# Weaving the second block's attention into its dense products by another measure, and turning stick-breaking weights from fp32r copies

## The chip, the cores and the metric

The kernel runs on one core of one Trainium2 chip. Its time is the device time of one launch in microseconds (us): median 1038.97 us over three runs (1035.66 to 1039.84). Each profile is one execution on the chip, taken by the hardware profiler. Five engines work side by side: TensorE (PE in the rows, PEld for its weight loads), VectorE (DVE), ScalarE (ACT), GpSimd (POOL) and SyncE (SP), which here only issues transfers. Each works through its own instructions in order.

## The reference

Two transformer-like blocks on a sequence of 512 tokens, width 1024, all in float32. The change touches the attention of the second block alone:

```python
h = rmsnorm_2(x, g_norm1) * (1.0 + sc1) + sh1
q_sb, k_sb, v_sb, q_ca, k_ca, v_ca = split(h @ w_in)
# 8 heads of stick-breaking attention, in blocks of 128 queries
z = einsum('bqhd,bkhd->bhqk', qb, kb) * d ** -0.5
log_1m_beta = where(strict, log_sigmoid(-z), 0.0)
suffix = cumsum(log_1m_beta, reverse=True) - log_1m_beta
w = where(strict, exp(log_sigmoid(z) + suffix), 0.0);  o_sb = w @ v
# 8 heads of banded softmax attention with a relative bias
q_ca, k_ca = rmsnorm_2(q_ca), rmsnorm_2(k_ca)
o_ca = softmax(q_ca @ k_ca * d ** -0.5 + bias) @ v
x = x + gt1 * (concat(o_sb, o_ca) @ w_o)
```

The factors sh1, sc1, gt1 and their later twins are slices of `silu(c) @ w_ada + b_ada`, a product of one row with a 1024 x 6144 matrix: the modulation. Everything in the block reads x, which the first block makes.

## The kernel before

A float32 weight is split into two fp32r halves, `wh` and `wl` (a cast on ScalarE, line 133, and a subtraction on GpSimd or VectorE, line 130), and each dense product is three matrix products (lines 152 to 154). The dense work of the second block is a generator, `dense2`: the q and k columns of one pair of heads after the other (`qk2_sb`, `qk2_ca`), two chunks of v (`v2_chunk`), and at last the products with w_o (`wo_first`), in the order of the table `DENSE`. The attention is a second generator, `attn2`. It goes through the 8 pairs of heads in the order 0, 1, 4, 2, 5, 3, 6, 7; pairs 0 to 3 are stick-breaking, 4 to 7 softmax. Each pair is 8 units: two heads, each with four query blocks i = 0 to 3, whose rows hold 128, 256, 384 and 512 keys.

A stick-breaking unit (`stick`) takes its scores z on TensorE (lines 452, 453, and a mask product, 960), goes through three ScalarE passes (lines 961 to 963), three VectorE passes (964, a reversed running sum in 966, 967) and an exponential on ScalarE (968). A softmax unit (`soft`) takes a VectorE pass (975), an exponential (977) and a scaling (978, 979). The `turn` of a unit, three units later (`LAG`), transposes its blocks on TensorE (line 987, in float32), and ScalarE or VectorE copies the result (990, 992). After a pair's last turn `pv2` multiplies by v (923).

TensorE's order is fixed by hand, by the planner `weave`: it keeps a clock, lets each stream go on only when what it asked for is ripe (`LAT_...`), and among the ready streams picks the one with the least `spent / share`. Both streams charge the TensorE time of what they issue; the share of attention is `SHARE2 = 0.55`. A gate keeps dense work at most two pairs ahead of attention. The order on the other engines is set by a scheduler from the dependencies.

The modulation comes in eighths: `ada` loads two row blocks of 512 KB and adds them up on VectorE (lines 219 and 221, 16 operations for the slice gt1, v = 2), called by `ada_step` after every attention unit until the list is done; `ada_end` closes a half on TensorE (238).

Of the kernel before, what the change touches and what calls it, by code (L numbers as in the profile page):

```python
# [9 lines left out]
F32R = mybir.dt.float32r  # L10
# [16 lines left out]


SHARE1 = 0.35
SHARE2 = 0.55  # L30
TURN2 = 4
TURN1 = 4
WOUT_DVE = (1, 2, 4, 6)
ORDER = (0, 1, 4, 2, 5, 3, 6, 7)
LAST_SB = 3
DENSE = (1, "v2", 4, 2, 5, 3, "v3", 6, 7)
LAT_CA = 6000.0
LAT_SM = 3200.0
LAT_SB = (4000.0, 5500.0, 6500.0, 7500.0)
LAT_CM = (3200.0, 3800.0, 4400.0, 5000.0)  # L40
LAT_QK = 2600.0
LAT_SQ = 5000.0
LAT_ADA = 6500.0
# [5 lines left out]
def f(ap):  # L49
    return ap.bitcast(F32)  # L50
# [3 lines left out]
def hybrid_then_adaln_block(ctx, tc, a, out, tap=None):  # L54
    nc = tc.nc
    pe, act, dve, pool, sp = nc.tensor, nc.scalar, nc.vector, nc.gpsimd, nc.sync

    consts = ctx.enter_context(tc.tile_pool(name="consts", bufs=1))
# [6 lines left out]
    def bank():  # L65
        return pbank.tile([128, 512], F32, name="ps", tag="ps", bufs=8)
# [4 lines left out]
    clk = [0.0]  # L71

    def mark(name, late=LAT_QK):
        done[name] = clk[0] + late
# [4 lines left out]
    def ripe_at(need):  # L79
        if need is None:  # L80
            return 0.0
        return need[1] if need[0] == "@" else done.get(need, float("inf"))

    def weave(*streams):


        share, streams = [x[0] for x in streams], [x[1] for x in streams]
        n = len(streams)
        spent, need, live = [0.0] * n, [None] * n, [True] * n
        while any(live):  # L90
            up = [q for q in range(n) if live[q]]
            ready = [q for q in up if ripe_at(need[q]) <= clk[0]]
            if not ready:
                clk[0] = min(ripe_at(need[q]) for q in up)
                assert clk[0] < float("inf"), need
                continue
            q = min(ready, key=lambda q: spent[q] / share[q])
            need[q] = None
            try:
                got = next(streams[q])  # L100
            except StopIteration:
                live[q] = False
                continue
            if isinstance(got, tuple):
                need[q] = got
            else:
                spent[q] += got
                clk[0] += got
# [4 lines left out]
    def sm(shape, name, bufs=4):  # L113
        return small.tile(shape, F32, name=name, tag=name, bufs=bufs)
# [53 lines left out]
    pool.memset(eps_c, EPS)  # L168
    ident = consts.tile([128, 128], F32, name="ident")
    make_identity(nc, ident)  # L170
    ones_f = consts.tile([128, 128], F32, name="ones_f")
    pool.memset(ones_f, 1.0)
    sel = consts.tile([128, 8], F32R, name="sel")
# [87 lines left out]
    def ada_step(n=1, wait=True):  # L261
        for _ in range(n):
            if ada_due and (clk[0] >= ada_due[0][2] or not wait):
                ada_end()
            if todo and not (ada_due and todo[0][1] % 4 == 0):
                ada(*todo.pop(0))
# [11 lines left out]
    def wt(shape, tag, dt=F32):  # L278
        return work.tile(shape, dt, name=tag, tag=tag, bufs=BUFS[tag])
# [199 lines left out]
    def attn1():  # L479
# [60 lines left out]
        for n in range(len(units) + LAG + 1):  # L540
            if n < len(units):
# [3 lines left out]
                yield scores(p, i, e)  # L545
                ripe[n] = clk[0] + LAT_SM
            if 0 <= n - LAG < len(units):
# [207 lines left out]
    for t in range(4):  # L755
        x = resid.tile([128, D], F32, name="xr", tag="xr", bufs=4)
# [160 lines left out]
    def pv2(p, W):  # L917
        po = bank()
        for j in range(4):
            n = 512 - 128 * j  # L920
            for e in range(2):
                hc = slice(128 * p + 64 * e, 128 * p + 64 * e + 64)
                pe.matmul(po[64 * e:64 * e + 64, 128 * j:], V2[j][:, hc], W[e][:, j, 128 * j:], start=j == 0, stop=j == 3)  # L923
            yield 0.89 * n
        if MX.get(p // 4) is not None:
            act.copy(MX[p // 4][:, p % 4, :], po)
        else:
            x = wt([128, 512], "T")
            act.copy(x, po)
            sp.dma_start(mx_d[p % 4], x)  # L930
            away.append(p % 4)
        mark(("mx", p), 1500.0)

    away = []
    st, P = {}, {}
# [10 lines left out]
    def att2_steps():  # L946
        def products(p, i, e, stop):
            if i == 0:
                st[p, e] = wt([128, 4, 512], "PT"), wt([128, 4, 512], "Y") if p < 4 else None
            L = 128 * (i + 1)  # L950
            N = max(L, 256)
            ps = bank()
            mm_packed(ps[:, :N], QK2[p], e, slice(128 * i, 128 * i + 128), slice(0, N), stop)
            x = P[p, i, e] = st[p, e][1][:, i, :] if p < 4 else wt([128, 512], "T")
            return ps[:, :L], x[:, :L], 2 * N / 2.4

        def stick(p, i, e):

            z, x, t = products(p, i, e, False)
            pe.matmul(z[:, 128 * i:], identb, mkb, start=False, stop=True)  # L960
            act.activation(x, z, AF.Abs)
            act.activation(x, x, AF.Exp, scale=-1.0)
            act.activation(x, x, AF.Ln, bias=1.0)
            dve.scalar_tensor_tensor(x, z, 0.0, x, op0=OP.max, op1=OP.add)
            back = x[:, ::-1]
            dve.tensor_tensor_scan(back, ones_f[:, :1].to_broadcast([128, z.shape[1]]), back, 0.0, op0=OP.mult, op1=OP.add)  # L966
            dve.tensor_tensor(x, z, x, op=OP.subtract)
            act.activation(x, x, AF.Exp)
            return t + 56

        def soft(p, i, e):
            s, x, t = products(p, i, e, True)
            nmx, sums = sm([128, 1], "nmx"), sm([128, 1], "sums")
            bs = strips[2 * (p - 4) + e]
            dve.tensor_tensor_reduce(x, s, bs[:, 384 - 128 * i:512], scale=-1.0, scalar=3.0e38,
                                     op0=OP.add, op1=OP.min, accum_out=nmx)
            act.activation(x, x, AF.Exp, scale=-1.0, bias=nmx, accum_out=sums)
            dve.reciprocal(sums, sums)
            dve.tensor_scalar(x, x, sums, None, op0=OP.mult)
            return t  # L980

        def turn(p, i, e):
            x = P.pop((p, i, e))
            PT = st[p, e][0]
            pt = bank().rearrange("p (j n) -> p j n", j=4)
            for j in range(i + 1):
                pe.transpose(pt[:, j, :], x[:, 128 * j:128 * j + 128], ident)  # L987
            o = PT[:, :i + 1, 128 * i:128 * i + 128]
            if i % 2:
                act.copy(o, pt[:, :i + 1, :])  # L990
            else:
                dve.tensor_copy(o, pt[:, :i + 1, :])
            return 110 * (i + 1)

        return stick, soft, turn

    def attn2():
        MX[0] = wt([128, 4, 512], "V")
        stick, soft, turn = att2_steps()
        units = [(p, i, e) for p in ORDER for e in range(2) for i in range(4)]  # L1000
        LAG = 3
        ripe = {}
        for n in range(len(units) + LAG + 1):
            if n < len(units):
                p = units[n][0]
                if n % 8 == 0:
                    yield ("qk2", p)
                yield (stick if p < 4 else soft)(*units[n])
                ada_step()
                ripe[n] = clk[0] + (LAT_SB if p < 4 else LAT_CM)[units[n][1]]  # L1010
                if n % 8 == 7:
                    mark(("att", p), 800.0)
            if 0 <= n - LAG < len(units):
                yield at(ripe[n - LAG])
                yield turn(*units[n - LAG])
            m = n - LAG - 1
            if m >= 0 and m % 8 == 7:
                p = units[m][0]
                yield at(clk[0] + LAT_PV2)
                yield from pv2(p, [st[p, e][0] for e in range(2)])  # L1020
                if p == LAST_SB:
                    MX[1] = wt([128, 4, 512], "Y")
                    for q in away:
                        sp.dma_start(MX[1][:, q, :], mx_d[q])

    def dense2():
        load_strips(0, f(h2l[1][:, 3, 384:385]))
        jobs = {"v2": lambda: v2_chunk(2), "v3": lambda: v2_chunk(3)}
        for x in DENSE:
            yield from with_norms(jobs[x]() if x in jobs else qk2_sb(x) if x < 4 else qk2_ca(x - 4))  # L1030
# [34 lines left out]
    for c in range(2):  # L1065
        for t in range(2, 4):
            run(v2_tile(c, t, vw[c]))
    weave((SHARE2, attn2()), (1.0, dense2()))
    if tap: tap("sb1", MX[0][:, 1, :]); tap("ca1", MX[1][:, 1, :])
# [23 lines left out]
    for t in range(4):  # L1093
        x = resid.tile([128, D], F32, name="xr", tag="xr", bufs=4)
# [37 lines left out]
    got = {}  # L1132
# [63 lines left out]
    for tag, n in [("PT", 1), ("Y", 1), ("V", 1), ("Y", 3), ("h", 2)]:  # L1196
        for _ in range(n):
            t = wt([128, 4, 512], tag) if tag != "h" else hpool.tile([128, 4, 512], F32, name="hid", tag="h", bufs=4)
# [202 lines left out]
```

## Time and profile before

| | |
|---|---|
| median of three runs | 1038.97 us |
| the profiled execution | 1035.2 us |
| its span, first to last instruction | 1033.5 us |
| TensorE, VectorE, ScalarE busy | 999.8, 654.9, 567.1 us |
| mean granted TensorE clock | 0.992 of full speed |

The profiled execution is 3.8 us below the median of the runs; 1.7 us of it lie outside the span. The page gives, for each engine, the share of the span in which it was busy. Since it is a mean over stages, the stage that the change touches (443 to 656 us, from the first stick-breaking scores to the last pair's product with v) is read by itself below.

### The profile page before, as it was taken

The numbers are of one execution on the slowest core, as the hardware profiler recorded it, in microseconds if no ns is written. First come the engines' busy times: TensorE is split into PE (matmuls) and PEld (weight loads), VectorE is DVE, ScalarE is ACT, GpSimd is POOL, SyncE is SP. The second block draws the span as 40 slices with busy tenths as digits, with TensorE's granted clock in tenths as the row PEclk, the third lists the DMA queues.
The fourth block names the chain that finished last, engine by engine and source line by source line (L and its number), as shares of the span: only waits on it lengthen the run. The fifth ranks groups of instructions, "written<-read, shape, count | busy, mean of one in ns | idle before, by whom it ended". The sixth has DMA issues, their size and how long they took to land.

```text
span 1033.5 us, 15410 instructions
## 1 busy us (share of the span) xinstructions
PE 999.8 (97%) x5870; PEld 850.0 (82%) x5870; DVE 654.9 (63%) x1204; ACT 567.1 (55%) x1098; POOL 294.5 (28%) x136
## 2 busy tenths in 40 slices
PE   8999999999999999997999989999999999999997
PEld 7987877868888888976777867799999998888886
DVE  5465867964636669678678778669578746611114
ACT  5456654445455455566689888347567773322330
POOL 4222214313333066003212134122122232333320
PEclk9999999999999999998999999999999999999999
DMA  8442534435455675335222244432244335732302
GB/s 232 121 143 62 139 97 123 122 113 153 112 153 163 218 230 166 99 102 164 67 68 81 72 129 128 147 104 81 55 111 123 85 128 175 194 112 84 101 20 82
DMA packets 136060, 125.55 MB, mean 121 GB/s; under 512 B 8141, under 2 KB 112417, under 8 KB 135986
## 3 DMA queue, kind: packets, MB, share of 16 engines
q1 hardware_dynamic: 135986, 124.56, 41.2%
q8 instruction: 46, 0.75, 0.3%
q14 instruction: 28, 0.23, 0.1%
HBM read 119.82 MB, written 4.73 MB: 121 GB/s over the span
## 4 chain that ended last, share of the span: by engine, by line
PE 83%; DVE 7%; ACT 5%; issue 3%; POOL 1%; DMA 1%; DVEq 0%; POOLq 0%; ACTq 0%
PE ps L152 21%; PE ps L153 20%; PE ps L154 20%; PE ps L1184 4%; PE ps L1186 4%; PE ps L1185 4%; PE ps L987 2%; PE ps L923 1%; PE ps L452 1%; PE ps L453 1%; DVE ada L221 1%; PE ps L533 1%; PE ps L515 1%; PE ps L238 1%; DVE Y L966 1%
## 5 line engine op out<-in xcount | busy, mean ns | idle before, releaser
L130 POOL TENSOR_TENSOR wl<-wr,wh 128x1024 fp32r<-128x1024 f32 x99 | 247.4, 2502 | 616.9 <-ACT wh L133 611.7
L133 ACT CAST wh<-wr 128x1024 fp32r<-128x1024 f32 x130 | 135.8, 1047 | 103.4 <-PE ps L153 40.5
L152 PE MATMUL ps<-hh,wh 128*128 128x512 f32 (+1 forms) x352 | 129.8, 369 | 0.0
L153 PE MATMUL ps<-hl,wh 128*128 128x512 f32 (+1 forms) x352 | 125.0, 355 | 0.0
L154 PE MATMUL ps<-hh,wl 128*128 128x512 f32 (+1 forms) x352 | 124.8, 355 | 0.0
L152 PE MATMUL ps<-wh,T 128*128 128x512 f32 x256 | 100.4, 392 | 0.0
L153 PE MATMUL ps<-wl,T 128*128 128x512 f32 x256 | 100.3, 392 | 0.0
L154 PE MATMUL ps<-wh,T 128*128 128x512 f32 x256 | 99.9, 390 | 0.0
L221 DVE SCALAR_TENSOR_TENSOR ada<-wr,vc,ada 128x512 f32<-128x512 f32 x84 | 83.0, 988 | 6.4 <-DMA wr<-in_w_ada_dram 5.1
L152 PEld LDWEIGHTS ps<-hh,wh 128*128 128x128 f32 x352 | 66.3, 188 | 19.7 <-issue 10.8
L154 PEld LDWEIGHTS ps<-hh,wl 128*128 128x128 f32 x352 | 66.4, 189 | 9.7
L153 PEld LDWEIGHTS ps<-hl,wh 128*128 128x128 f32 x352 | 66.4, 189 | 7.7
L154 PEld LDWEIGHTS ps<-wh,T 128*128 128x128 f32 x256 | 48.1, 188 | 10.8
L152 PEld LDWEIGHTS ps<-wh,T 128*128 128x128 f32 x256 | 48.1, 188 | 10.6
L153 PEld LDWEIGHTS ps<-wl,T 128*128 128x128 f32 x256 | 48.1, 188 | 10.2
L130 DVE TENSOR_TENSOR wl<-wr,wh 128x1024 fp32r<-128x1024 f32 x31 | 40.9, 1319 | 24.1 <-ACT wh L133 24.0
L152 PE MATMUL ps<-h2h,wh 128*128 128x512 f32 (+1 forms) x144 | 54.3, 377 | 0.0
L1186 PE MATMUL ps<-QK,wl 128*128 128x256 f32 x192 | 53.6, 279 | 0.0
L1184 PE MATMUL ps<-QK,wh 128*128 128x256 f32 x192 | 53.5, 279 | 0.0
L1185 PE MATMUL ps<-PT,wh 128*128 128x256 f32 x192 | 53.3, 278 | 0.0
L154 PE MATMUL ps<-h2h,wl 128*128 128x512 f32 (+1 forms) x144 | 52.9, 367 | 0.0
L153 PE MATMUL ps<-h2l,wh 128*128 128x512 f32 (+1 forms) x144 | 52.7, 366 | 0.0
(412 smaller groups left out, 2687.1 us busy)
## 6 DMA issues: line engine op xcount, KB each, us to landing
wr<-in_w_in_dram SPq DMA_DIRECT2D x64, 512.0 KB, 4.7
wr<-in_w_dram SPq DMA_DIRECT2D x64, 512.0 KB, 4.1
wr<-in_w_ada_dram SPq DMA_DIRECT2D x48, 512.0 KB, 4.4
wr<-in_w_out_dram SPq DMA_DIRECT2D x12, 512.0 KB, 4.3
wr<-in_w_o_dram SPq DMA_DIRECT2D x12, 512.0 KB
xr<-in_x_dram SPq DMA_DIRECT2D x8, 512.0 KB
wr<-in_w_up_pool_dram SPq DMA_DIRECT2D x8, 256.0 KB
wr<-in_w_up_attn_dram SPq DMA_DIRECT2D x8, 256.0 KB, 4.2
```

Of the source, the lines that this page charges most:

```text
L130: (eng or pool).tensor_tensor(dst, raw, f(hi), op=OP.subtract)
L133: act.copy(dst_hi, raw)
L152: pe.matmul(ps, lh, rh, start=start, stop=False, **go)
L153: pe.matmul(ps, lh, rl, start=False, stop=False, **go)
L154: pe.matmul(ps, ll, rh, start=False, stop=stop, **go)
L221: dve.scalar_tensor_tensor(acc, raw[:, q, :], cs, acc, op0=OP.mult, op1=OP.add)
L238: pe.matmul(ps[:, j:j + 1], acc[:, 128 * j:128 * j + 128], ones_f[:, :1], start=True, stop=True)
L452: pe.matmul(ps, A[e][:, sa], B[e][:, sb], start=True, stop=False)
L987: pe.transpose(pt[:, j, :], x[:, 128 * j:128 * j + 128], ident)
L1184: pe.matmul(ps, wh, bh, start=first and k == 0, stop=False, **go)
L1185: pe.matmul(ps, wh, bl, start=False, stop=False, **go)
L1186: pe.matmul(ps, wl, bh, start=False, stop=k == 3, **go)
```

## The change

Five things are edited. The shares and delays of the planner change. A unit of attention now advances the clock by its TensorE time as before, but charges its stream a pace by block (`PACE_SB` 1100 to 2900 ns, `PACE_CM` 750 to 1600 ns), the turns charge nothing, and the share is 0.8. The second v chunk moves behind pair 6 in `DENSE`. The modulation waits until the seventeenth unit and takes a step at every third unit. And the weights of a stick-breaking unit are copied after their exponential, by a transfer from one SBUF tile to another of type fp32r (a third tile per head of the tag `Y`, whose four buffers stay); the turn reads the copy with an fp32r identity.

```diff
-SHARE2 = 0.55
+SHARE2 = 0.8
+PACE_SB = (1100.0, 1700.0, 2300.0, 2900.0)
+PACE_CM = (750.0, 1000.0, 1300.0, 1600.0)
...
-DENSE = (1, "v2", 4, 2, 5, 3, "v3", 6, 7)
+DENSE = (1, "v2", 4, 2, 5, 3, 6, "v3", 7)
...
-LAT_SB = (4000.0, 5500.0, 6500.0, 7500.0)
-LAT_CM = (3200.0, 3800.0, 4400.0, 5000.0)
+LAT_SB = (6500.0, 8000.0, 9000.0, 10000.0)
+LAT_CM = (4500.0, 5000.0, 5500.0, 6500.0)
...
-            if isinstance(got, tuple):
+            if isinstance(got, tuple) and got[0] == "$":
+                clk[0] += got[1]
+                spent[q] += got[2]
+            elif isinstance(got, tuple):
                 need[q] = got
...
+    identr = consts.tile([128, 128], F32R, name="identr")
+    dve.tensor_copy(identr, ident)
...
-            yield 0.89 * n
+            yield "$", 0.89 * n, 100.0
...
-                st[p, e] = wt([128, 4, 512], "PT"), wt([128, 4, 512], "Y") if p < 4 else None
+                st[p, e] = [wt([128, 4, 512], "PT")] + ([wt([128, 4, 512], "Y"), wt([128, 4, 512], "Y", F32R)] if p < 4 else [])
...
             act.activation(x, x, AF.Exp)
+            sp.dma_start(f(st[p, e][2][:, i, :z.shape[1]]), x)
...
-                pe.transpose(pt[:, j, :], x[:, 128 * j:128 * j + 128], ident)
+                c = slice(128 * j, 128 * j + 128)
+                if p < 4:
+                    pe.transpose(pt[:, j, :].bitcast(F32R), st[p, e][2][:, i, c], identr)
+                else:
+                    pe.transpose(pt[:, j, :], x[:, c], ident)
...
-                yield (stick if p < 4 else soft)(*units[n])
-                ada_step()
+                t = (stick if p < 4 else soft)(*units[n])
+                yield "$", t, (PACE_SB if p < 4 else PACE_CM)[units[n][1]]
+                if n >= 16 and n % 3 == 0:
+                    ada_step()
...
-                yield turn(*units[n - LAG])
+                yield "$", turn(*units[n - LAG]), 0.0
```

What moves is shown at three places. The first is VectorE at the very start of the stage, the first head of pair 0; `Y` are a unit's values, `ada` the running sum of the modulation. Before:

```order
L964 SCALAR_TENSOR_TENSOR Y_4324<-ps_4325,Y_4324 128x128
L246 SCALAR_TENSOR_TENSOR scl_91<-mod_90,vc_89 128x4
L219 TENSOR_SCALAR ada_4366<-wr_4364,vc_89 128x512
L966 SCALAR_TENSOR_TENSOR Y_4324<-ones_f_83,Y_4324 128x128
L221 SCALAR_TENSOR_TENSOR ada_4366<-wr_4364,vc_89,ada_4366 128x512
L967 TENSOR_TENSOR Y_4324<-ps_4325,Y_4324 128x128
L964 SCALAR_TENSOR_TENSOR Y_4324<-ps_4369,Y_4324 128x256
L221 SCALAR_TENSOR_TENSOR ada_4366<-wr_4383,vc_89,ada_4366 128x512
L966 SCALAR_TENSOR_TENSOR Y_4324<-ones_f_83,Y_4324 128x256
L221 SCALAR_TENSOR_TENSOR ada_4366<-wr_4383,vc_89,ada_4366 128x512
L967 TENSOR_TENSOR Y_4324<-ps_4369,Y_4324 128x256
L964 SCALAR_TENSOR_TENSOR Y_4324<-ps_4387,Y_4324 128x384
```

The same place in the changed kernel, whose lines 964, 966 and 967 are 972, 974 and 975:

```order
L972 SCALAR_TENSOR_TENSOR Y_4326<-ps_4328,Y_4326 128x128
L974 SCALAR_TENSOR_TENSOR Y_4326<-ones_f_85,Y_4326 128x128
L975 TENSOR_TENSOR Y_4326<-ps_4328,Y_4326 128x128
L972 SCALAR_TENSOR_TENSOR Y_4326<-ps_4367,Y_4326 128x256
L974 SCALAR_TENSOR_TENSOR Y_4326<-ones_f_85,Y_4326 128x256
L975 TENSOR_TENSOR Y_4326<-ps_4367,Y_4326 128x256
L972 SCALAR_TENSOR_TENSOR Y_4326<-ps_4388,Y_4326 128x384
L449 SCALAR_TENSOR_TENSOR QK_4350<-ps_4357,QK_4350 64x512
```

No operation of the modulation stands among the first units any more; the packing of the next pair's q (line 449) comes between them.

The second place is VectorE inside pair 4, at the change from its first head to its second; `T` are a softmax unit's values and `Z` the bias strips. Before (line 975 is the first pass of a softmax unit, 978 and 979 its scaling, 992 a copy after a turn):

```order
L975 ISA T_5062,nmx_5063<-ps_5059,Z_4336 128x512
L975 ISA nmx_5063 128x1
L978 RECIPROCAL sums_5048<-sums_5048 128x1
L992 COPY PT_5013<-ps_5075 128x128
L979 TENSOR_SCALAR T_5046<-T_5046,sums_5048 128x384
L942 MEMSET Z_5314 64x64
L978 RECIPROCAL sums_5064<-sums_5064 128x1
L979 TENSOR_SCALAR T_5062<-T_5062,sums_5064 128x512
L975 ISA T_5092,nmx_5093<-ps_5089,Z_4341 128x128
```

The changed kernel there, with lines 984, 987, 988, 1005 and 229 for 975, 978, 979, 992 and 221:

```order
L984 ISA T_5044,nmx_5045<-ps_5041,Z_4340 128x512
L984 ISA nmx_5045 128x1
L1005 COPY PT_4951<-ps_5051 128x128
L229 SCALAR_TENSOR_TENSOR ada_5032<-wr_5089,vc_91,ada_5032 128x512
L987 RECIPROCAL sums_5046<-sums_5046 128x1
L984 ISA T_5068,nmx_5069<-ps_5065,Z_4345 128x128
L984 ISA nmx_5069 128x1
L988 TENSOR_SCALAR T_5044<-T_5044,sums_5046 128x512
L984 ISA T_5082,nmx_5083<-ps_5079,Z_4345 128x256
L984 ISA nmx_5083 128x1
L229 SCALAR_TENSOR_TENSOR ada_5032<-wr_5089,vc_91,ada_5032 128x512
```

All 16 operations of the modulation now stand between the units of pairs 4, 2 and the first of pair 5.

The third place is SyncE's queue of transfers around pair 2; `wr` are weights, `Z` bias strips. Before:

```order
L139 DMA wr_5644<-in_w_in_2_dram 128x4x256
L139 DMA wr_5810<-in_w_in_2_dram 128x8x128
L139 DMA wr_5867<-in_w_in_2_dram 128x8x128
L139 DMA wr_5925<-in_w_in_2_dram 128x8x128
L944 DMA Z_5314<-in_band_dram 64x64
```

The changed kernel, where line 977 is the new copy of a unit's weights:

```order
L977 DMA Y_5129<-Y_5128 128x128
L217 DMA wr_5609<-in_w_ada_2_dram 128x2x512
L145 DMA wr_5631<-in_w_in_2_dram 128x8x128
L145 DMA wr_5690<-in_w_in_2_dram 128x4x256
L951 DMA Z_5205<-in_band_dram 128x448
L951 DMA Z_5210<-in_band_dram 128x448
L952 DMA Z_5210<-in_band_dram 64x64
L977 DMA Y_5129<-Y_5128 128x256
```

The 32 copies share the queue with the loads; the second copy of pair 2 stands behind six of them.

## Rows read from the trace of the kernel before

**Rows 1.** The page: span, and busy time of each engine.

```profile
span 1033.5 us, 15410 instructions
PE 999.8 (97%) x5870; PEld 850.0 (82%) x5870; DVE 654.9 (63%) x1204; ACT 567.1 (55%) x1098; POOL 294.5 (28%) x136
```

**Rows 2.** Windows: length, each engine's busy time (instructions), clock, DMA share, GB/s.

```profile
443.00:520.50 77.50, 67.72 (x386) 56.38 (x385) 58.16 (x95) 54.01 (x112) 20.91 (x8) 0.96 0.41 116
520.50:568.30 47.80, 47.39 (x280) 36.79 (x278) 39.71 (x106) 42.81 (x98) 8.96 (x4) 1.00 0.23 72
568.30:650.70 82.40, 75.40 (x416) 59.45 (x414) 64.99 (x151) 65.56 (x140) 25.23 (x10) 0.98 0.37 113
```

**Rows 3.** TensorE's waits, 443 to 656 us: total, times, longest.

```profile
PE ps L453 <- DVE lz L448: 4.4, 1, 4.4
PE ps L238 <- DVE Y L967: 2.5, 1, 2.5
...
PE ps L987 <- DVE T L979: 1.7, 1, 1.7
```

**Rows 4.** TensorE's waits, 443 to 521 us.

```profile
PE ps L152 <- ACT V L828: 2.7, 2, 1.9
```

**Rows 5.** TensorE's timeline: start, length, line, operation, out<-in, shape, [wait].

```profile
440.85 0.28 PE L152 MATMUL ps<-Y,h2h 128*128 128x256 f32 x1
440.96 0.28 PE L153 MATMUL ps<-Y,h2h 128*128 128x256 f32 x1
...
474.24 0.67 PE L452 MATMUL ps<-QK 128*128 128x384 f32 x1
...
520.17 0.60 PE L987 MATMUL ps<-ident,Y 128*128 128x128 f32 x4
...
567.94 0.60 PE L987 MATMUL ps<-ident,T 128*128 128x128 f32 x4
...
588.62 0.39 PE L152 MATMUL ps<-h2h,wh 128*128 128x512 f32 x1
588.85 0.39 PE L153 MATMUL ps<-h2l,wh 128*128 128x512 f32 x1
...
649.80 0.93 PE L987 MATMUL ps<-ident,T 128*128 128x128 f32 x7
```

**Rows 6.** VectorE by line, 443 to 493 us: count, total busy, mean ns.

```profile
L221 DVE SCALAR_TENSOR_TENSOR ada<-wr,vc,ada 128x512 f32<-128x512 f32 x14 | 14.4, 1031 | 0.1
L219 DVE TENSOR_SCALAR ada<-wr,vc 128x512 f32<-128x512 f32 x2 | 0.9, 470 | 0.0
```

**Rows 7.** VectorE's timeline at 447 and 455 us.

```profile
447.19 0.74 DVE L221 SCALAR_TENSOR_TENSOR ada<-wr,vc,ada 128x512 f32<-128x512 f32 x1
447.85 0.68 DVE L966 TENSOR_TENSOR_SCAN Y<-ones_f,Y 128x256 f32<-128x256 f32 x1
...
454.93 2.79 DVE L221 SCALAR_TENSOR_TENSOR ada<-wr,vc,ada 128x512 f32<-128x512 f32 x1
457.64 0.68 DVE L967 TENSOR_TENSOR Y<-ps,Y 128x512 f32<-128x512 f32 x1
```

**Rows 8.** The window of the first three heads.

```profile
443.00:493.00 50.00, 40.22 (x254) 33.59 (x253) 43.12 (x75) 34.65 (x80) 12.13 (x4) 0.93 0.48 137
```

**Rows 9.** The chain that ended last, at 477 and 643 us: start, length, what.

```profile
477.39 0.77 PE ps L987 x4
...
643.13 0.44 PE ps L987 x4
```

**Rows 10.** Transfers, 443 to 656 us: count, KB each, us from issue to landing.

```profile
Y<-mx_d SPq DMA_DIRECT2D x2, 256.0 KB, 3.7
...
Z<-in_band_dram SPq DMA_DIRECT2D x6, 16.0 KB, 2.9
```

**Rows 11.** SyncE's waits, 443 to 656 us.

```profile
SPq L139 <- POOL wl L130: 73.4, 16, 11.1
SPq L209 <- DVE Y L967: 17.8, 1, 17.8
...
SPq L943 <- DVE Z L942: 12.6, 2, 9.1
```

**Rows 12.** Longest forms of a softmax unit, 442 to 656 us: count, total, mean ns.

```profile
L979 DVE TENSOR_SCALAR T<-T,sums 128x512 f32<-128x512 f32 x8 | 5.8, 724 | 0.2
L975 DVE CUSTOM_DVE_ANT_0 T<-ps,Z 128x512 f32<-128x512 f32 x8 | 5.4, 679 | 1.2 <-PE ps L453 1.2
```

**Rows 13.** The same on ScalarE.

```profile
L977 ACT ACTIVATE T<-T,nmx 128x512 f32<-128x512 f32 x8 | 5.8, 722 | 1.0 <-DVE nmx L975 1.0
```

More of the change, by code (lines that the diff above doesn't have):

```diff
@@ L35 @@
 LAST_SB = 3
-DENSE = (1, "v2", 4, 2, 5, 3, "v3", 6, 7)
+DENSE = (1, "v2", 4, 2, 5, 3, 6, "v3", 7)
 LAT_CA = 6000.0
-LAT_SM = 3200.0
-LAT_SB = (4000.0, 5500.0, 6500.0, 7500.0)
-LAT_CM = (3200.0, 3800.0, 4400.0, 5000.0)
+LAT_SM = 4000.0
+LAT_SB = (6500.0, 8000.0, 9000.0, 10000.0)
+LAT_CM = (4500.0, 5000.0, 5500.0, 6500.0)
 LAT_QK = 2600.0
```

## The prediction

> **What bounds the kernel now.** The page comes first: TensorE is busy 999.8 of 1033.5 us [rows 1], so only a stage in which it is not can give much. The windows come next, cut where the same unit's turn ends, because these marks exist in both orders: first scores at 443.0, the last turn of pair 1 ends near 520.5, that of pair 5's first head near 568.3, the last turn of all near 650.7 [rows 5]. Call the stretches A, B and C. In A TensorE is busy 67.7 of 77.5 us at a mean clock of 0.96, in B 47.4 of 47.8, in C 75.4 of 82.4 at 0.98 [rows 2]. So B is bound by TensorE and loses nothing; A is the place with the loss. The list of waits names it: 4.4 us for the packing of the next pair's k on VectorE, 2.5 us behind a stick-breaking unit on VectorE, 2.7 us for copies of v [rows 3, 4]. The clock adds to it: score products of 384 columns that take 0.67 us at 474 us [rows 5] run at the lower level (1.2 GHz) behind the 4.4 us pause; 0.04 of 77.5 us at a loss is 3.1 us. Why is VectorE late there? In the first 50 us it is busy 43.1 [rows 8], and the 14 additions and 2 products of the modulation, 14.4 + 0.9 us, stand among its units [rows 6].
>
> **The change, part by part.** The sums are against the profiled execution's own 1035.2 us (1033.5 of span and 1.7 outside), which is 3.8 us below the median of 1038.97; I add the 3.8 at the end.
>
> *Products moved.* By the emitted order A held 150 dense products of 512 columns and 96 of 256, and now holds 156 and 96; B 90 and 36, now 96 and 0; C 168 and 60, now 168 and 96. A 512-column product starts 0.23 us after the one before, a 256-column one 0.11 to 0.12 [rows 5]. So A gains 6 x 0.23 = 1.4 us of work, B gets 1.4 and loses 36 x 0.118 = 4.2, so -2.9, C gets 4.2. Twelve 512-column products that stood behind the last turn are now ahead of it, so C's mark has 2.7 us less behind it: C counts 4.2 - 2.7 = +1.5. That nets to zero, as it must.
>
> *A, the modulation leaves.* VectorE's work there falls from 58.2 us busy by the 16 operations. Their price has two ends: 0.66 us from start to start where they run freely (447.19 to 447.85 [rows 7]), so 16 x 0.66 = 10.6, and the 15.3 us of their rows [rows 6], in which one of 2.79 us stands [rows 7]. Either way VectorE is left with 43 to 48 us beside 69 us or so of TensorE work: it stops setting the pace. I take the two VectorE waits (6.9) and the clock (3.1) as gone, 10.0; the waits for v copies stay. Next late is a weight copy: the exponential of the second head's first unit in pair 1 stands behind a copy of the unit turned just before it, and its transfer must then land; 2.5 us of that show on TensorE. With 1.4 of more products and the turns below: -10.0 + 1.4 + 2.5 - 1.5 = -7.6. Bounds: -11 if no copy is late, -2 if half the waits stay.
>
> *The turns.* Four float32 transposes take 0.44 us at the full clock, 0.11 each [rows 9]. An fp32r turn is not in the trace. It cannot save more than what a product of 128 columns at the 256-column rate would, 0.055 of 0.11: 80 x 0.055 = 4.4 us over four pairs, if TensorE sets the pace throughout; it can save nothing if the load of the weights sets the step. Half of A's 40 at that rate is about 1.1; I take 1.5 in A and nothing in B and C, where TensorE waits. The Trainium skill (TensorE: Matmul & The Clock Gate, Terms) says that a transpose has a mode of its own that is four times faster for FP32. It speaks against a gain from the type, and the rows agree so far that 0.11 us per float32 transpose is no more than a 256-column fp32r product takes; by it the term is 0 and the total 1.5 us higher.
>
> *B, the modulation arrives.* VectorE was busy 39.7 of 47.8 us there beside a TensorE that never waited [rows 2]. The 16 operations add 10.6 to 15.3, so 50.3 to 55.0, while TensorE's work falls to 47.8 - 2.9 = 44.9. The same units, packs and copies stand between the two marks on VectorE in both orders, so this is a bound by order, not a mean. VectorE cannot be full: in the first 50 us, where it set the pace, it was busy 43.1, or 86% [rows 8]. I take 52.5 at 93%, 56.5 us: +8.7. Bounds: -2.9 if the operations hide after all, +16 with 55.0 at 86%.
>
> *The weight copies.* Each of 32 units gets a transfer of 64 to 256 KB on SyncE's queue, between exponential and turn. From issue to landing 16 KB took 2.9 us and 256 KB 3.7 [rows 10]. Where dense products stand between scores and turn this is covered. Where attention stands alone (the second half of pair 2, the first head of pair 3) three units are in flight and about a third of 3.3 us per unit shows. In B VectorE is the later one already, so I cost it at nothing there; in C two places of half a landing, 2 x 1.6 = 3. The copies are also queued behind loads that wait: SyncE waited up to 11.1 us for a weight buffer and 9.1 for a strip [rows 11], and the second copy of pair 2 stands behind two strips. That is a rival below. The Trainium skill (DMA: Bandwidth & Descriptors, Anatomy of one DMA) says that a transfer has a fixed cost of about 2 us, mostly the receipt of the last write, so small ones do not get cheap; the trace agrees in kind, 16 KB takes most of what 256 KB takes. By that figure alone the two places would cost 2 x 1.0 = 2 us, one less than here.
>
> *C.* +1.5 of products and +3 of copies. The last pair's turns now stand in one row without dense products ahead of its product with v, so its last unit's chain shows: 0.68 + 0.72 + 0.72 and the small steps between, some 2.5 us [rows 12, 13], where 1.7 us of such a wait stood before [rows 3]: +1. C lost 7.0 us of idle time [rows 2], of which the later place of the v chunk may free 2. So +3.5; bounds -4 and +10.
>
> The sum: -7.6 + 8.7 + 3.5 = +4.6. The rest of the program is untouched. 1035.2 + 4.6 = 1039.8, and with the 3.8 us 1043.6 for a median of runs.
>
> **The rivals.** *B's queue hides* (faster). If the scheduler's order lets the modulation fill VectorE's 8.1 idle us of B [rows 2], B costs +1 by its 50.3, C nothing: -7.6 + 1 + 0 = -6.6, 1032.4. For it speaks that VectorE had that idle time; against, that TensorE's turns need the operations behind it in order.
>
> *The copies queue behind loads* (slower). SyncE issues in order. If strips and weights that wait for buffers hold back the copies of pairs 2 and 3, each of some five held copies shows a landing and a half, 5 x 5 = 25 us, less what B's VectorE bound already has (8): 1039.8 + 17, or 1061 with the 3.8. It decides from the point at which such a load waits more than the copy's slack of about 3 us; the waits of 9.1 and 11.1 [rows 11] speak for it, that they stood in a queue with nothing urgent behind it speaks neither way.
>
> *Loss and gain cancel.* With B at 52 us (+4.2) and C at +2 the sum is -1.4, 1037.6. Under it the modulation is merely moved.
>
> **How the numbers follow.** About 0.5%, 5.2 us, can be told from no change here. Forecast 0.42, in its own range 1039 to 1049, and split evenly by the line at 1044.2; queue hidden 0.22; copies held 0.18; cancelled 0.18. So faster 0.22, same 0.21 + 0.18 = 0.39, slower 0.21 + 0.18 = 0.39. The range takes in the faster rival down to 1030 and most of the held copies up to 1060; the bounds of the terms, -11 - 2.9 - 4 and -2 + 16 + 10, lie outside it together, since they would have to meet.
>
> **What would show it.** In the changed profile A should last 70 us with a clock near 1.00 and no wait of several us for VectorE; B 56 with VectorE busy over 50 of it and the clock perhaps below 1.00; C 86. TensorE's waits in B should name VectorE lines of the units. If they name the transfers of line 977, the copies are the bound; if the rows of line 998 start 0.06 us apart, the turns are faster. The forecast is wrong if B stays under 50 us, or if A keeps a wait of 4 us.

## The result, and the profile after

The changed kernel takes 1062.7 us (median of four runs, 1061.1 to 1064.1) against 1038.5 for the kernel before: a ratio of 1.025, 95% interval 1.0221 to 1.028. It is slower by 24 us, 19 us above the forecast and 2.7 us beyond its range. The page of the changed kernel begins like this; it answers to [rows 1]:

```profile
span 1062.3 us, 15520 instructions
PE 1012.8 (95%) x5870; PEld 854.9 (80%) x5870; DVE 653.7 (62%) x1205; ACT 571.7 (54%) x1098; POOL 291.7 (27%) x136
```

VectorE and ScalarE are busy about as long as before. TensorE has no more products to do, yet is busy 13.0 us longer. The windows, cut at the same turns as [rows 2], say where (length, busy time of TensorE, its weight loads, VectorE, ScalarE and GpSimd, granted clock, DMA share, GB/s):

```profile
440.80:510.70 69.90, 64.17 (x377) 52.91 (x376) 47.59 (x84) 55.62 (x116) 12.14 (x5) 1.00 0.30 91
510.70:578.30 67.60, 54.09 (x255) 39.84 (x255) 53.05 (x116) 42.29 (x94) 10.19 (x4) 0.85 0.43 132
578.30:680.50 102.20, 86.71 (x458) 67.25 (x457) 63.69 (x151) 67.03 (x139) 25.60 (x10) 0.92 0.36 108
```

A is 69.9 us instead of 77.5, B 67.6 instead of 47.8, C 102.2 instead of 82.4: together 32.0 us longer. (The span grew by 28.8: the first scores come 2.2 us sooner in this execution, and 1.0 us less stands behind the last turn.) Add up TensorE's busy time: 190.5 before, 205.0 now. So of the 32.0 us, 17.5 are idle and 14.5 are products that ran longer (the 2.7 us of products moved ahead of the mark and what the turns save nearly cancel), at a mean clock of 0.85 in B and 0.92 in C where [rows 2] have 1.00 and 0.98. TensorE's waits in B and then in C (total, times, longest):

```profile
PE ps L460 <- DVE nmx L984: 3.4, 1, 3.4
PE ps L998 <- ACT PT L1003: 3.3, 1, 3.3
PE ps L1000 <- DVE T L988: 2.7, 2, 2.0
PE ps L998 <- ACT Y L970: 2.5, 1, 2.5
```

```profile
PE ps L998 <- DMA Y<-Y: 5.1, 3, 2.2
PE ps L1000 <- DVE T L988: 4.1, 3, 1.7
PE ps L998 <- DVE Y L974: 2.3, 1, 2.3
```

All but the first are turns (998, 1000); line 460 is the score products of a softmax unit. Only 5.1 us are put down to the copies (`Y<-Y`), but the list names whatever ended last, and that need not be what the turn needed. Here are the issue of a copy and the turn that reads it, with its wait in brackets:

```profile
612.29 0.47 SPq L977 DMA_DIRECT2D Y<-Y  x1
615.04 0.26 PE L998 MATMUL ps<-identr,Y 128*128 128x128 f32 x1 [2.27 <-DVE Y L974]
```

By the trace's semaphore updates this copy landed at 614.91 us, and the pass of line 974 that is named belongs to another unit. The three turns that the list does put down to copies start 0.14 us behind a landing; so does this one, and so do the turns at 496.39 (a wait of 2.4 us, put down to line 972) and 545.87 (2.5 us, line 970). Six turns thus wait for landings, 12.3 us in all: 2.4 in A, 2.5 in B, 7.3 in C.

The chain of waits shows how they spread; here it is through the first head of pair 3 (start, length, what):

```profile
605.79 0.31 ACT Y L976
...
606.13 2.81 DMA Y<-Y
608.94 0.14 issue
609.08 0.26 PE ps L998
...
609.36 0.29 DVE PT L1005
609.65 0.48 DVE Y L972
...
614.36 0.63 ACT Y L976
...
615.01 2.28 DMA Y<-Y
617.30 0.14 issue
617.43 0.64 PE ps L998 x4
```

An exponential ends, its copy takes 2.8 us to land, the turn follows, VectorE copies the turn's result (1005), and only behind that copy, in VectorE's order, stands the first pass (972) of a later unit. So a late landing delays that unit's values as well, and with them its copy. The chain is a ring, and TensorE stands in it.

A second chain, in pair 2, has no copy in it:

```profile
526.00 0.67 DVE ada L229
526.67 0.02 issue
526.69 5.52 DMA wr<-in_w_in_dram
532.22 0.02 issue
532.24 1.05 ACT wh L139
```

A modulation step still holds a raw weight buffer, the load that needs it is issued behind it, and ScalarE stands before the cast of that load (3.9 us by its list of waits), with a turn's result and a unit's first passes queued behind.

What the order gave TensorE to do meanwhile can be counted in it. Between the scores of the second, third and fourth unit of pair 2's first head and their turns stood 18, 15 and 21 dense products of 512 columns; now 3, 0 and 0. In pair 3's first head the changed order has 3, 0 and 0 as well, where the one before had 30 and 33 of 256 columns, then 9 of 512 and 27 of 256.

### The profile page after: what moved, and what is told of

The parts are those of the page before. It is cut to its first block, busy times and chain, and to the rows that moved or that the text cites. A ratio compares the mean times of both kernels' runs of the same rounds, so it can differ in the third digit from the quotient of the medians.

```text
span 1062.3 us, 15520 instructions
## 1 busy us (share of the span) xinstructions
PE 1012.8 (95%) x5870; PEld 854.9 (80%) x5870; DVE 653.7 (62%) x1205; ACT 571.7 (54%) x1098; POOL 291.7 (27%) x136
## 4 chain that ended last, share of the span: by engine, by line
PE 72%; DVE 11%; ACT 6%; issue 5%; DMA 4%; POOL 2%; DVEq 0%; SPq 0%; POOLq 0%; ACTq 0%
PE ps L158 18%; PE ps L159 17%; PE ps L160 17%; PE ps L1199 4%; PE ps L1201 4%; PE ps L1200 4%; DMA wr<-in_w_out_dram 2%; PE ps L931 2%; DVE ada L229 2%; ACT wh L139 1%; PE ps L541 1%; PE ps L460 1%; DVE Y L974 1%; DVE Y L136 1%; PE ps L461 1%
## 5 line engine op out<-in xcount | busy, mean ns | idle before, releaser
L136 POOL TENSOR_TENSOR wl<-wr,wh 128x1024 fp32r<-128x1024 f32 x99 | 244.6, 2474 | 655.2 <-ACT wh L139 655.2
L229 DVE SCALAR_TENSOR_TENSOR ada<-wr,vc,ada 128x512 f32<-128x512 f32 x84 | 86.2, 1026 | 6.3 <-DMA wr<-in_w_ada_dram 4.9
```

The costliest lines, as they stand in the source:

```text
L136: (eng or pool).tensor_tensor(dst, raw, f(hi), op=OP.subtract)
L229: dve.scalar_tensor_tensor(acc, raw[:, q, :], cs, acc, op0=OP.mult, op1=OP.add)
```

## The experiments

Each line is the median of its own runs; the ratio is to runs of the kernel before on the same chip, with its 95% interval. "Held" is the modulation held back, "new weave" the planner's numbers and charges. The kernel before took 1038.5 us beside the changed kernel and 1036.6 to 1036.9 beside the others, so two lines are compared below by their distances from the kernel before; the intervals leave 1.5 to 4.5 us to either side of each.

| run | what it is | us | ratio |
|---|---|---|---|
| e3 | new weave alone | 1040.1 | 1.0043 (1.0017 to 1.0069) |
| e1 | new weave, held | 1047.9 | 1.0128 (1.0086 to 1.017) |
| e2 | new weave, copy | 1052.6 | 1.0181 (1.0139 to 1.0222) |
| after | new weave, held, copy | 1062.7 | 1.025 (1.0221 to 1.028) |
| e8 | held alone | 1036.6 | 0.9988 (0.9973 to 1.0003) |
| e7 | copy alone | 1038.8 | 1.0018 (0.9999 to 1.0038) |
| e10 | copy, new latencies | 1039.9 | 1.0031 (1.0011 to 1.0052) |
| e11 | copy, new paces | 1052.7 | 1.017 (1.013 to 1.021) |
| e4 | after, copies on ScalarE's queue | 1055.9 | 1.0219 (1.0175 to 1.0263) |
| e5 | after, copies not read | 1049.0 | 1.0121 (1.0088 to 1.0154) |
| e6 | after, no copy, fp32r turns | 1049.2 | 1.0115 (1.009 to 1.0141) |
| e9 | after, four units in flight | 1042.7 | 1.0062 (1.0037 to 1.0087) |
| e13 | new weave, copy, four | 1039.2 | 1.002 (1.0006 to 1.0034) |
| e14 | new weave, held, four | 1043.2 | 1.0065 (1.0041 to 1.0089) |
| e15 | new weave, four | 1039.3 | 1.0022 (1.0004 to 1.0041) |
| e12 | before, held, four | 1044.9 | 1.0084 (1.0041 to 1.0128) |

**What each part costs.** e1 takes the copy out and has float32 turns:

```diff
-            sp.dma_start(f(st[p, e][2][:, i, :z.shape[1]]), x)
...
-                    pe.transpose(pt[:, j, :].bitcast(F32R), st[p, e][2][:, i, c], identr)
+                    pe.transpose(pt[:, j, :], x[:, c], ident)
```

> The changed kernel without the copy: no transfer of the weights, no fp32r tile, the stick-breaking turns read the float32 weights as before. TensorE's order stays that of the changed kernel. Its median is 1062.7 us. Theory COPIES (the transfers wait on SyncE's queue for their exponentials, 70 us of that queue's waits between 440 and 690 us, hold weight loads behind them and land late): most of the loss goes, 1040 to 1046. Theory HELD (the modulation's operations, pushed into pairs 4, 2 and 5, fill VectorE and keep raw weight buffers, so a load is issued late at 526.7 us and ScalarE stands still behind its cast until 532): only the landings that TensorE shows go, 5.1 us and the half clock after them, so 1055 to 1058. Theory WEAVE (the new pace and latencies leave attention alone without dense products, whatever else is there): also 1055 to 1060.

e2 calls the modulation as before, e3 does both:

```diff
-                if n >= 16 and n % 3 == 0:
-                    ada_step()
+                ada_step()
```

> The changed kernel with the modulation called after every unit, as before; copies and weave stay. HELD: the stretch from pair 1's last turn to pair 5's first head falls from 67.6 us to about 50, the one before it grows from 69.9 to about 76, so about 1051. COPIES: the held loads and landings stay, the first stretch gets worse, 1062 to 1068. WEAVE: 1062 to 1067.

> Only the weave is left of the change: its shares, paces, latencies and place of the v chunk; no copy, float32 turns, modulation after every unit. WEAVE: still slow, 1052 or more, with waits of TensorE of several us in pairs 2, 3 and 6. COPIES or HELD: 1036 to 1042, the kernel before within half a per cent.

None of the theories alone: e1 came out 2 us above what COPIES had, e2 near what HELD had, and e3 rules WEAVE out as the whole. The weave by itself costs about 4 us, holding the modulation 8 more (e1 against e3, and after against e2), the copy 12.5 (e2 against e3) to 13 (after against e1). The three add up to the 24, so what had to be explained is why copy and holding are dear. The second chain above belongs to the holding: e1, without a copy, has it too (ScalarE stands 2.8 us before that cast), and e3 does not.

**The copy: queue, landing or buffers?** e4 issues it on another queue:

```diff
-            sp.dma_start(f(st[p, e][2][:, i, :z.shape[1]]), x)
+            act.dma_start(f(st[p, e][2][:, i, :z.shape[1]]), x)
```

> The changed kernel with each copy issued on ScalarE's own queue, just behind the exponential that writes the weights, so that nothing on SyncE's queue stands behind it; all else is the same, and TensorE's order with it. COPIES by way of the queue: weight loads come as early as without the copy, 1042 to 1048 (landings still show, 5 us). COPIES by way of the landing alone, HELD, WEAVE: 1058 to 1064.

It falls between the two theories: 5 of 13 us come back, or 3 by the ratios, whose intervals overlap, so the gain is not clear of the noise. On SyncE's queue a copy that waits for its exponential holds what is behind it. SyncE's waits in the changed kernel, 536 to 566 us, and its issues there, the longest wait standing ahead of the copy at 560.39 and of two weight loads:

```profile
SPq L977 <- ACT Y L976: 10.0, 3, 5.9
SPq L977 <- ACT Y L969: 5.5, 2, 5.3
```

```profile
553.94 0.47 SPq L977 DMA_DIRECT2D Y<-Y  x1
560.39 0.47 SPq L977 DMA_DIRECT2D Y<-Y  x1
562.35 1.01 SPq L145 DMA_DIRECT2D wr<-in_w_in_dram  x2
```

In e4 the same two loads are issued from 551.92 on, held by nothing but buffers:

```profile
551.92 5.47 SPq L145 DMA_DIRECT2D wr<-in_w_in_dram  x2
```

e5 leaves the copies where they are and turns the float32 weights; e6 has no transfer, and the exponential writes the fp32r tile:

```diff
-            act.activation(x, x, AF.Exp)
-            sp.dma_start(f(st[p, e][2][:, i, :z.shape[1]]), x)
+            act.activation(st[p, e][2][:, i, :z.shape[1]], x, AF.Exp)
```

> The changed kernel with the copies still issued on SyncE's queue into their tiles, but the turns read the float32 weights, so no turn waits for a landing. The runs so far put the copy at 15 us (1062.7 with it, 1047.9 without), and 7 of them at SyncE's queue (1055.9 with the copies on ScalarE's). Theory LANDING (the other 8 are the turns that wait 1.4 to 2.7 us for a transfer, five or six times, with the half clock behind): 1053 to 1056, with about 7 us over the kernel without copies left for the queue. Theory BUFFERS (the other 8 are the second weight tile of each head, which takes two of the four buffers of its kind): 1060 to 1063. If queue and landing are the same loss seen twice: 1048 to 1050.

> The changed kernel with no transfer at all: the exponential writes the weights straight into the fp32r tile (rounded to that type), the turns read it in fp32r; the second tile of each head stays. LANDING and queue: 1044 to 1048, the time without the copy less up to 2.4 us for 80 turns at 0.08 instead of 0.11 us. BUFFERS: 1053 to 1056.

e5 settles it: with all 32 copies still in the queue, but nobody waiting for them, the time is 1049.0, the same within the intervals as without them. And the queue is held there too: between 437 and 690 us SyncE's waits for ScalarE at line 977 add up to 65.6 us in e5 and 74.6 in the changed kernel. So holding the queue costs nothing that these runs can tell; what costs is the turns that wait for landings. I had set 1053 to 1056 for landing plus queue; it came out as if the two were one loss seen twice. What e4 gained, if it gained, stays unexplained; ScalarE issues the copies there, and no run parts that from the rest. e6, 1 us above its own range, clears the buffers.

**Why did the old weave not pay?**

> The kernel before with the copy and the fp32r turns alone; its own weave and its modulation after every unit. If the copy's price is its own (12.5 us beside the new weave and the old modulation): 1048 to 1053. If the new latencies covered part of it, the old weave with its turns sooner behind the scores pays more: 1055 to 1065. If the copy hurts only in the new weave: 1036 to 1041.

> The kernel before with copy, fp32r turns and the new latencies (LAT_SM, LAT_SB, LAT_CM); its shares, its charging by TensorE time, its place of the v chunk and its modulation after every unit stay. The copy alone took 1038.8. If the latencies are what makes the copy dear: 1048 to 1054. If the shares and paces do it: 1036 to 1041, the later turns hiding the nine waits for landings of the copy alone (9.1 us).

> The other half: copy and fp32r turns with the new share, paces and turns that charge nothing; latencies, the place of the v chunk and the modulation as before. If the paces make the copy dear: 1048 to 1054. If the latencies do: 1037 to 1043.

e7 is the kernel before with the copy lines and the fp32r turns; e10 adds the new `LAT_...` numbers to it; e11 is the changed kernel with the old latencies, `DENSE` and modulation. The paces make the copy dear, the latencies don't. (No run has the paces without the copy and without the new latencies; that most of e11's loss is the copy's is taken from e3, where the whole weave costs 4 us.) The counts of products go with it: for the same three units of pair 2 they are 18, 15 and 21 in e7, 24, 27 and 27 in e10, and 3, 0 and 0 in e11. e7's turns do wait for landings:

```profile
its engine sat idle before it (us, times) until:
  DMA Y<-Y: 9.1, 9
```

That is more than the 5.1 that this list gives the changed kernel, in nine pieces of at most 2.0 us, and yet the kernel is only 2 us slower. Six of the nine fall in A, and there TensorE is idle for 9.6 us in e7 and 9.8 in the kernel before: they stand in the place of other waits. The paces pack a head's units together and put the dense products behind the head, 48 in a row.

**The depth.**

```diff
-        LAG = 3
+        LAG = 4
```

> The changed kernel with each unit's turn emitted four units after its scores instead of three; nothing else. If the copy costs because three units in flight are too few to cover its landing where attention stands alone: most of the copy's 14 us come back, 1048 to 1053. If the loss there is one chain around the engines' orders, not the depth: 1058 to 1066.

> The changed kernel with turns four units behind and the modulation after every unit as before; weave and copy stay. With three units the held modulation cost 8 to 10 us beside the new weave. If it is VectorE's and the weight buffers' own price, whatever the depth: 1032 to 1036, faster than both kernels. If it was the same loss as the copy's, seen through the pauses of the three-unit pipeline: 1040 to 1045.

> The changed kernel with turns four units behind and no copy (float32 turns); the modulation stays held. If the copy's price was the depth alone: 1042 to 1046, as with it (1042.7), or up to 2 us above for the dearer turns. If the copy still costs in buffers or queue: 1035 to 1039.

> The new weave alone with turns four units behind: no copy, modulation after every unit. At three units it took 1040.1, 3.5 more than the kernel before. If the weave's own loss (TensorE waiting for exponentials 4.1 us and for quotients 4.6 us) is depth too: 1031 to 1035. If not: 1038 to 1042.

With the turn a fourth unit behind, 18 to 20 us of 24 come back (e9), more than either theory had. Its windows, between the same turns:

```profile
437.60:511.20 73.60, 67.58 (x379) 55.60 (x378) 51.34 (x89) 54.84 (x116) 12.28 (x5) 0.95 0.28 86
511.20:567.40 56.20, 48.54 (x257) 36.80 (x256) 51.50 (x112) 40.54 (x92) 10.09 (x4) 0.94 0.47 150
567.40:657.30 89.90, 80.16 (x457) 63.28 (x456) 64.58 (x150) 65.13 (x139) 24.17 (x10) 1.00 0.43 128
```

C is 12.3 us shorter and its clock is back at 1.00; only 0.8 us of waiting for a landing is left, in B. At this depth the copy costs nothing (e13 against e15: 1039.2 and 1039.3; e9 against e14: 1042.7 and 1043.2), and holding the modulation 3.5 to 4 instead of 8. So the copy's price was depth altogether, the modulation's by about half; the other half stays at this depth. More dense products are only part of what the fourth unit brings: of the three units of pair 2 counted above, two still have 3 and 0 of them in e9, and the third has 48. The weave's own loss is not depth, as far as the intervals tell (e15 against e3: 1039.3 and 1040.1). For e13 I had expected 1032 to 1036 or 1040 to 1045, and neither came.

**Holding the modulation, in the old weave.**

```diff
-                ada_step()
+                if n >= 16 and n % 3 == 0:
+                    ada_step()
```

> The kernel before with the modulation held back alone (from the 17th unit, every third). As the prediction's terms have it: -10 in the first two pairs, +8.7 in pairs 4 and 2, so 1036 to 1039. As the runs of the new weave have it (7.8 us for the same edit without copies): 1044 to 1048.

> A version that might beat both: the kernel before with the modulation held back (1036.6 alone) and the turns four units behind. If the waits that are left in pairs 3, 6 and 7 are units whose chain is longer than three units cover: 1029 to 1034. If a fourth unit only moves products about: 1035 to 1040.

e8's windows are the cleanest test of two terms of the prediction:

```profile
439.60:509.00 69.40, 65.09 (x370) 53.71 (x369) 47.12 (x73) 51.76 (x108) 12.94 (x6) 0.98 0.18 54
509.00:563.90 54.90, 50.18 (x285) 39.14 (x286) 48.61 (x120) 42.91 (x99) 8.92 (x4) 0.98 0.36 111
563.90:648.80 84.90, 78.91 (x422) 61.49 (x422) 67.24 (x157) 65.10 (x142) 24.71 (x10) 0.95 0.41 129
```

A is 8.1 us shorter, B 7.1 and C 2.5 longer, and the time is that of the kernel before: the work is merely moved. e12 missed both of its ranges: a fourth unit makes the old weave 8 us slower than e8, which I have not explained. So depth paid in the new weave, and did not in the old. No run beats the kernel before; e8's interval reaches past 1.

## Why the prediction was wrong, point by point

**The step that failed: each edit was priced beside the old order.** Sorted by edit, the forecast has -1.0 us for the weave (1.4 - 2.9 + 1.5 of products moved, +1 and -2 in C), +1.6 for the held modulation (-10.0 in A, and in B from 44.9 to 56.5) and +4.0 for copies and turns (2.5 - 1.5 + 3). Alone beside the kernel before, the three cost 3.5, -0.1 and 2.1 us (e3, e8, e7): 5.5 together, near the 4.6 of the forecast, though for the weave not even the sign was right. But beside the new weave the held modulation costs 8 and the copy 12.5 to 13. The sum had no term for this: the new order takes away the products that stood between scores and turns, and a turn one unit deeper gives back all of the copy's price and half of the modulation's (e9 and e13 to e15).

**A (-7.6, 70 us, clock near 1.00)** came out to the tenth: 69.9 us against 77.5, at 1.00, with VectorE busy 47.6 where I had 43 to 48. The tenth is luck, since the first scores, from which A is counted, come anywhere from 437.5 us (e5) to 443.0 (before). The copy that I had as late by 2.5 us is there: it is the wait of 2.4 us at 496.39, of the very unit named. But the reason for the rest was only half right. The new weave alone, with the modulation still there, already brings A to 72.1; e1, with both, has 72.0:

```profile
439.10:511.20 72.10, 68.29 (x394) 56.65 (x393) 62.25 (x101) 53.68 (x113) 14.89 (x6) 0.98 0.38 111
511.20:563.60 52.40, 47.00 (x248) 35.42 (x247) 39.56 (x101) 42.16 (x95) 7.19 (x3) 0.97 0.21 66
563.60:657.20 93.60, 83.23 (x450) 64.64 (x449) 61.00 (x149) 65.81 (x139) 25.27 (x10) 0.96 0.35 104
```

```profile
439.30:511.30 72.00, 66.55 (x377) 55.07 (x376) 48.77 (x87) 55.32 (x117) 12.40 (x5) 0.98 0.18 52
511.30:569.30 58.00, 49.30 (x255) 36.71 (x254) 49.05 (x112) 40.78 (x91) 10.88 (x4) 0.94 0.46 132
569.30:664.30 95.00, 83.77 (x459) 65.14 (x457) 61.45 (x153) 65.90 (x140) 25.42 (x10) 0.96 0.35 102
```

The first fence is e3, the second e1. A's loss can be won once. Beside the new weave, holding the modulation gains nothing in A and pays 5.6 us in B, which is most of its 8.

**B (+8.7, bound by VectorE, 56 us).** Held alone it is +7.1, with VectorE busy 48.6 of 54.9 us and TensorE's two longest waits there, 1.9 and 1.6 us, put down to VectorE's scaling (979, 978): the mechanism and its size were right. With the whole change B is 67.6. The sentence that failed is "In B VectorE is the later one already, so I cost it at nothing there": from e1 to the changed kernel the copy adds 9.6 us to B. Half of it, 4.8, is idle time of TensorE, in which one landing shows with 2.5; the other half is products that ran longer. VectorE, busy 53.1 of 67.6 us, was not simply the bound. That the rest is the ring of turn, VectorE and transfer, seen above in pair 3, is argued and not shown for B.

**C (+3.5).** It came to +19.8. The weave alone gives 93.6 us, +11.2, of which I had moved products of 4.2. The held modulation adds 1.4. The copy adds 7.2 where I had two half landings, 3; its four waits for landings in C are 7.3.

**Products moved, "that nets to zero, as it must".** This step failed in kind. I counted how many products changed places and priced them by their own length; I did not count how many stayed between a unit's scores and its turn. The counts above (18, 15, 21 against 3, 0, 0) were in the emitted order, and in e7, e10 and e11 the copy's price goes with them. I had written that "a third of 3.3 us per unit shows" where attention stands alone, and that was near: of the eight units in the first heads of pairs 2 and 3, four wait 7.6 us for landings, 1.0 a unit. But the sum did not use it; it has 0 in B and 3 in C, and nothing for the clock. [rows 5] had the sign of that last term: products of 384 columns at 0.67 us behind a pause. In the changed kernel 540 to 550 us, amid the stops of pair 2, has a mean of 0.67, between the two levels of 1.2 and 2.4 GHz:

```profile
530.00:540.00 10.00, 5.13 (x21) 2.67 (x21) 6.57 (x14) 7.44 (x15) 0.00 (x0) 0.78 0.48 136
540.00:550.00 10.00, 7.51 (x39) 5.88 (x35) 5.45 (x12) 5.85 (x15) 0.00 (x0) 0.67 0.27 95
```

I priced waits by their length alone; here the slower products cost nearly as much again (14.5 beside 17.5).

**The rival with held copies (1061)** was near in time and wrong in place. In pair 2 the second copy is issued at 539.93 us, as its exponential ends, and no load had held it. It is the copies that hold the loads, and e5 shows that even this costs nothing by itself.

**The turns (1.5 us).** A turn of four in fp32r (second row) and one of a single transpose (first row):

```profile
453.62 0.22 PE L998 MATMUL ps<-identr,Y 128*128 128x128 f32 x1
...
467.44 0.46 PE L998 MATMUL ps<-identr,Y 128*128 128x128 f32 x4
```

That is (0.46 - 0.22) / 3 = 0.08 us from one transpose to the next, against 0.11 [rows 9]: 80 x 0.03 = 2.4 us at most, inside my 0 to 4.4. So the type does matter here. e6 against e1 shows none of it in the time (1049.2 and 1047.9).

**What stays open**: which part of the weave's own 2 to 4 us is the place of the v chunk and which the paces; what the copies on ScalarE's queue gain; how the copy makes B 9.6 us longer with one landing of 2.5 us in it; and why four units harm the old weave.

## What to carry to other kernels

When an order changes, count for each dependent pair the independent work that stands between them, and compare that with the latency of the chain, before adding up what was moved. Here 32 transfers put into such a chain cost 12.5 to 13 us in an order that left 3, 0 and 0 products there, about 2 us in one that left 15 to 21, and nothing with the turn one unit deeper. An edit that costs nothing alone can be dear beside another, so price each beside the order that will stand around it. Two edits that remove the same loss earn it once. And a list of waits can name the wrong engine: where a turn reads what a transfer brings, compare its start with the landing.

## What the runs showed of the hardware

In the changed kernel an addition of the modulation took 0.74 us alone, but up to 2.8 beside GpSimd's subtraction, and a running sum of 128 columns 1.54 instead of 0.42 (at 603.90 us). There VectorE's four additions (first fence) ran beside two subtractions on GpSimd (second):

```profile
560.28 6.96 DVE L229 SCALAR_TENSOR_TENSOR ada<-wr,vc,ada 128x512 f32<-128x512 f32 x4
```

```profile
559.91 5.20 POOL L136 TENSOR_TENSOR wl<-wr,wh 128x1024 fp32r<-128x1024 f32 x2 [35.93 <-ACT wh L139]
```

They took 7.0 us instead of 3.0, and TensorE's wait of 3.4 us in B is behind them. The passes that read scores from PSUM showed no such rise (972 and 975 at 384 columns: 0.56 us alone and beside it). The Trainium skill (SBUF — State Buffer, Who interferes with whom) says that a VectorE instruction with two SBUF inputs contends with a GpSimd instruction that reads SBUF; these rows agree. So the 16 operations of the modulation have no fixed price: it depends on what GpSimd does where they are put.
